# Zero-padded filter operand, a later inverse transform, and GpSimd's share of the norm in a two-layer encoder

## The chip, the cores and the metric

The kernel runs on one core of one Trainium2 chip. The metric is the device time of one execution in microseconds (us): 1728.81 us before, the median of three runs between 1728.32 and 1731.26. Smaller is better.

## The reference

The reference is an encoder of two layers on 256 positions of 1024 channels, in float32. Each layer mixes tokens, adds the result to the stream and normalises, then mixes channels, adds and normalises again:

```
def hybrid_mixer(x, ...):
    proj = einsum('bsd,dp->bsp', x, w_in)                  # 8 x 1024 columns
    a_b, a_c, a_u, h_in, gate_logits = split(proj)
    y_a = a_b * dwconv3_centred(a_c * a_u, conv_a_w)
    h_in = dwconv3_centred(h_in, conv_h_w) + conv_h_b
    h_v, h_x1, h_x0 = split(h_in)
    k_fwd, k_bwd = implicit_filters(...)     # sin-FFN of positions @ w3, times a decay window, unit norm
    z = h_v * h_x1
    z = bidirectional_fft_conv(z, k_fwd, k_bwd) + z * hyena_bias
    y_h = h_x0 * z
    g_a, g_h = split(sigmoid(gate_logits))
    merged = g_a * (y_a @ w_a_out) + g_h * (y_h @ w_h_out)
    return merged @ w_o

def reference(x, ...):
    h = layer_norm(x, ln_in_g, ln_in_b)
    for l in range(2):
        h = layer_norm(ALPHA * h + hybrid_mixer(h, ...), ln_mix_g[l], ln_mix_b[l])
        f = swiglu(h, ...) if l == 0 else moe_swiglu(h, ...)    # dense, then top 2 of 8 experts
        h = layer_norm(ALPHA * h + f, ln_ffn_g[l], ln_ffn_b[l])
    return h
```

A layer_norm subtracts the mean over the 1024 channels, multiplies by 1/sqrt(variance + 1e-5), then by g, and adds b.

## The kernel before

**Matrix products.** Most products are made in three parts (`mm3`, L174 to L176): both operands are split into a rounded high part and a low remainder, and the three matmuls high x high, low x high and high x low add up in one PSUM bank. Weights arrive by SyncE's DMA queue in tiles `wt` of 1 MB. ACT writes the high half of each (L167), VectorE subtracts it for the low half (L168), into a ring `hl` of six tiles of 128x1024; the splitting runs up to five tiles ahead of TensorE. A *chunk* uses two of these tiles: 16 `mm3`, which is 48 matmuls of 128x256. The tiles are numbered here from the start of the kernel (tile 45, tile 46, ...).

**One layer's mixer.** After the norm, `to_T` transposes the 256x1024 stream on TensorE (L542, eight 128x128 blocks for each half `tt` of 128 positions), ACT and VectorE evict with gain and bias (L555, L552), and `hilo` makes the parts `xh` and `xl`. Then come chunks: the inputs of the Hyena branch first, then four `x0_chunk` and twelve `a_chunk`. The discrete Fourier transform of the Hyena branch, its product with the filter and the inverse transform are cut into events (`dft_a`, `dft_b`, `dft_c`, `idft`, each for half 0 or 1 of the channels), and a table `after` says behind which of these 16 chunks each event is issued: the offset `o` plus the place in a list. `dft_c` adds and subtracts on GpSimd and splits the four results on ACT and VectorE (L168, tile `big`). `idft` is 32 matmuls (L705 to L708) whose banks VectorE evicts (L711, L714). After the 16 chunks come four rounds of four chunks (gate, projection of y_a, gate, projection of y_h) and `w_o`.

**The filters.** `flt_c` is called eight times a layer. Each call makes two products of the hidden layer with `w3`: a matmul of 128 rows (L405: the high part twice, against the high and the low part of `w3`) and one of 64 rows (L406: the low part `fl` against the high part of `w3`), for each of the two directions. Layer 0's calls stand among its own chunks; layer 1's stand among layer 0's last chunks, in the stretch of the norm behind layer 0's mixer, and in layer 0's channel mixer.

**The norm.** For each half `tt`, VectorE makes the statistics (L485 to L489), GpSimd raises to -1/2 (L490, called pow below), VectorE applies mean and scale in two pieces of 128x512 (L497). `h_from_n` then makes the stream for the residual on GpSimd: a multiplication (L527) and an addition (L528) of 128x1024 for each `tt`. It does so under `tc.issue_after`, a context of the scheduler in which an instruction is put behind the named one. The norms are numbered by `i`: 0 of the input, 1 and 2 of layer 0, 3 and 4 of layer 1. `to_T` makes parts (`want_parts`) for norms 0 to 2; for norm 3 it does not, and issues `warm(8)` and `warm(2)` behind its two groups of transposes. `warm(n)` is n matmuls of a matrix of ones (L244, 128x512, bfloat16) into a bank that nobody reads.

The order of instructions on each engine is the order in which the program issues them, as a scheduler arranges it at build time.

Of the kernel before, what the change touches and what calls it, by code (L numbers as in the profile page):

```python
# [9 lines left out]
F32 = mybir.dt.float32  # L10
F32R = mybir.dt.float32r
BF16 = mybir.dt.bfloat16
I32 = mybir.dt.int32
U32 = mybir.dt.uint32
AF = mybir.ActivationFunctionType
ALU = mybir.AluOpType

P = 128
S = 256
# [146 lines left out]
def hilo(nc, hi, lo, src):  # L166
    a = nc.scalar.activation(hi, src, AF.Copy)  # L167
    v = nc.vector.tensor_tensor(out=lo, in0=src, in1=hi.bitcast(F32), op=ALU.subtract)  # L168
    return a.ins, v.ins
# [44 lines left out]
def body(tc, nc, x, vec, rows, fg, winT, zT, fw1, fw2, fb, fw3, w_in, w_ao, w_ho, w_o, w13, w2,  # L214
         m13, m2, cst, out, dbg=None):
# [7 lines left out]
    def mm_bank(shape=(P, 2, 256)):  # L223
        t = psum.tile(list(shape), F32, name="mm", tag="mm", bufs=3)
        return t

    def acc_bank(shape=(P, 512)):
        t = psum.tile(list(shape), F32, name="acc", tag="acc", bufs=4)
        return t
# [5 lines left out]
    def warm(n, after=None):  # L235

        if not n:
            return
        t = mm_bank([P, 4, P])
        with ExitStack() as st:  # L240
            if after is not None:
                st.enter_context(tc.issue_after(after.ins))
            for _ in range(n):
                nc.tensor.matmul(t, ones_b, ones_b[:, None, :].to_broadcast([P, 4, P]), start=True, stop=True)  # L244
# [7 lines left out]
    xp = mix.enter_context(tc.tile_pool(name="xp", bufs=1))  # L252
    tmp = mix.enter_context(tc.tile_pool(name="tmp", bufs=10))

    def big8(shape, dt=F32):
        t = big.tile(list(shape), dt, name="big", tag="big")
        return t

    def t2k(shape=(P, 2, 256), dt=F32):
        t = tmp.tile(list(shape), dt, name="t2k", tag="t2k")  # L260
        return t
# [31 lines left out]
    W = Weights(tc, nc, wts, hls, 3, NH - 1)  # L293
# [40 lines left out]
    W.load(3)  # L334
    ff = xp.tile([P, 2, 4, P], F32R)
    gg = xp.tile([P, 4, 2, P], F32R)
    fg_raw = big8([P, 2, 4, P])
    nc.sync.dma_start(fg_raw, fg)

# [17 lines left out]
    def flt_bank(l, shape=(P, 2, 256)):  # L357
        return acc_bank(shape) if l == 0 else mm_bank(shape)

    def flt_h(l, which):  # L360

        n = 64 * (1 + which)
        if which == 0:
            flt_load(l, 0)
            flt_load(l, 1)
            lhs, rhs = fw1_s[:, l], zT_s
        else:
            lhs, rhs = fw2_s[:, l], fs.pop((l, "h"))
        ps = flt_bank(l, [n, S])
        nc.tensor.matmul(ps, lhs, rhs, start=True, stop=True)  # L370
        t = xp.tile([n, S], F32, name="fh", tag="fh")
        sin_of((ps, t, 2 * which, n), l)
        if which == 0:
            fs[l, "h"] = t
        else:
            fs[l] = xp.tile([P, S], F32R, name="fr", tag="fr"), xp.tile([64, S], F32R, name="fl", tag="fl")
            nc.scalar.activation(fs[l][0], t, AF.Copy)
            nc.vector.tensor_tensor(out=fs[l][1], in0=t[:64], in1=fs[l][0][:64].bitcast(F32), op=ALU.subtract)

    def flt_load(l, ct):  # L380
        if ct < 8:
            wn = tmp.tile([P, S], F32, name="wn", tag="wn", bufs=3)
            nc.sync.dma_start(wn, winT[ct])
            w3 = tmp.tile([P, 2, P], F32, name="w3", tag="w3", bufs=2)
            nc.sync.dma_start(w3, fw3[l, ct])
            fs[l, "w", ct] = wn, w3

    def flt_w(l, ct):

        if (l, "w", ct) in fs:  # L390
            wn, w3 = fs.pop((l, "w", ct))
            wr = tmp.tile([P, 2, P], F32R, name="wr", tag="wr", bufs=2)
            with tc.issue_after(last["sina"].ins):
                nc.scalar.activation(wr, w3, AF.Copy)
            nc.vector.tensor_tensor(out=wr[64:], in0=w3[64:], in1=wr[64:].bitcast(F32), op=ALU.subtract)
            fs[l, "p", ct] = wn, wr
            flt_load(l, ct + 2)

    def flt_c(l, ct):

        flt_w(l, ct)
        wn, wr = fs.pop((l, "p", ct))
        ps = flt_bank(l)
        for s in range(2):
            nc.tensor.matmul(ps[:, s], wr[:, s], fs[l][0], start=True, stop=False)  # L405
            nc.tensor.matmul(ps[:, s], wr[:64, s], fs[l][1], start=False, stop=True)  # L406
        if ct != 4 or l == 0:
            flt_w(l, ct + 1)
        hw = t2k()
        nc.vector.tensor_tensor(out=hw, in0=ps, in1=wn[:, None, :].to_broadcast([P, 2, S]), op=ALU.mult)  # L410
        ss = small.tile([P, 2], F32, name="ss", tag="ss")
        sd = t2k()
        for s in range(2):
            nc.scalar.activation(sd[:, s], hw[:, s], AF.Square, accum_out=ss[:, s:s + 1])
        rn = small.tile([P, 2], F32, name="rn", tag="rn")
        nc.gpsimd.tensor_scalar(out=rn, in0=ss, scalar1=1e-6, scalar2=None, op0=ALU.add)
        nc.gpsimd.tensor_tensor(out=rn, in0=rn, in1=mhalf, op=ALU.pow)
        for s in range(2):
            nc.scalar.activation(hw[:, s], hw[:, s], AF.Copy, scale=rn[:, s:s + 1])
        nc.gpsimd.memset(hw[:, 1, 0:1], 0.0)  # L420
        for s, op in enumerate((ALU.add, ALU.subtract)):
            nc.gpsimd.tensor_tensor(out=sd[:, s], in0=hw[:, 0], in1=hw[:, 1], op=op)
        fs[l, "sd", ct] = sd
# [44 lines left out]
    fs = {}  # L468
# [10 lines left out]
    last = {}  # L479
# [42 lines left out]

    def h_from_n(i, n):
        g = gb.pop(i)
        with tc.issue_after(last["pow"].ins):
            for tt in range(2):
                nc.gpsimd.tensor_tensor(out=h_t[:, tt], in0=n[:, tt], in1=g[:, 0], op=ALU.mult)  # L527
                nc.gpsimd.tensor_tensor(out=h_t[:, tt], in0=h_t[:, tt], in1=g[:, 1], op=ALU.add)  # L528

    def to_T(i, n, want_parts=True):  # L530

        xf = big8([P, KT, S])
        xh = xl = None
        if want_parts:
            xh = hp.tile([P, KT, S], F32R, name="xh", tag="xh")
            xl = hp.tile([P, KT, S], F32R, name="xl", tag="xl")
        tbs = [acc_bank([P, 2, 2, P]) for _ in range(4)]
        for tt in range(2):
            for kp in range(4):
                for k in range(2):  # L540
                    kk = 2 * kp + k
                    ins = nc.tensor.transpose(tbs[kp][:, k, tt], n[:, tt, kk * P:(kk + 1) * P], id_s)  # L542
            if not want_parts:
                warm((8, 2)[tt], ins)
        for kp in range(4):
            tb = tbs[kp]
            k0 = 2 * kp
            for k in range(2):
                kk = k0 + k
                g, b = ln_g(i)[:, kk:kk + 1], ln_b(i)[:, kk:kk + 1]  # L550
                if kp % 2:
                    ev = nc.vector.tensor_scalar(out=xf[:, kk], in0=tb[:, k], scalar1=g, scalar2=b, op0=ALU.mult,  # L552
                                                 op1=ALU.add)
                else:
                    ea = nc.scalar.activation(xf[:, kk], tb[:, k], AF.Identity, bias=b, scale=g)  # L555
            if want_parts:
                W.after = hilo(nc, xh[:, k0:k0 + 2], xl[:, k0:k0 + 2], xf[:, k0:k0 + 2])
        if not want_parts:
            W.after = ea.ins, ev.ins
        return xf, xh, xl  # L560
# [40 lines left out]
    def mixer(l, xh, xl):  # L601
# [21 lines left out]
        for j in range(4):  # L623
            ps = proj(W.next(), xs)
# [7 lines left out]
            ps = proj(W.next(), xs)  # L632
# [111 lines left out]

        sts = [{} for _ in range(4)]
        chunks = [(x0_chunk, j) for j in range(4)] + [(a_chunk, j, w, sts[j]) for j, w in A_ORDER]
        o = 5 if l == 0 else 1
        after = {1: [(z_parts, 3)]}
        for q, ev in enumerate(([(dft_a, 0)], [(dft_b, 0, 0)], [(dft_b, 0, 1)], [(dft_a, 1), (dft_c, 0)], [(dft_b, 1, 0)],
                                [(dft_b, 1, 1), (idft, 0)], [], [(dft_c, 1)], [], [(idft, 1)])):  # L750
            after[o + q] = after.get(o + q, []) + ev
        for q, (f, *a) in enumerate(chunks):
            f(*a)
# [22 lines left out]
        for j in range(4):  # L776
            ps = proj(W.next(), xs)
# [3 lines left out]
            ps = proj(W.next(), yas)  # L781
            nc.vector.tensor_tensor(out=ga, in0=ps, in1=ga, op=ALU.mult)
            fill0()
            ps = proj(W.next(), xs)
# [3 lines left out]
            ps = proj(W.next(), yhs)  # L788
# [52 lines left out]
    xf, xh, xl = to_T(0, n_t)  # L841
    W.split(2)
    with W.behind():
        flt_h(0, 0)
# [9 lines left out]
    for l in range(DEPTH):  # L854
# [14 lines left out]
        if l == 0:  # L869
# [3 lines left out]
            xf, xh, xl = to_T(li, n_t)  # L873
# [16 lines left out]
            xf, xh, xl = to_T(li, n_t)  # L890
# [56 lines left out]
    ins = logits(1)  # L947
# [3 lines left out]
    with tc.issue_after(ins.ins):  # L951
        back = [turn_back(0, 1)]
        for tt in range(2):
            ins = nc.tensor.transpose(lgp[:, tt], lgs[:, tt * P:(tt + 1) * P], id_s[:NE, :NE])
# [246 lines left out]
    with tc.issue_after(last["oneh"].ins), tc.issue_after(cp.ins):  # L1201
        for tt in range(2):
            ins = h_half(tt, 1, back[tt])
# [27 lines left out]
    for r, v in enumerate(nc.values_load_multi_w_load_instructions(ix[0:1], engines=[mybir.EngineType.SP], min_val=0,  # L1231
# [4 lines left out]
                            in1=keys[:, None, :].to_broadcast([P, NE, NE]), op=ALU.is_equal)  # L1236
# [155 lines left out]
```

## Time and profile before

| | before |
|---|---|
| median of 3 runs | 1728.81 us (1728.32 to 1731.26) |
| the profiled execution | 1726.32 us |
| its span | 1724.4 us |
| TensorE (PE) busy | 1670.5 us, 97% |
| VectorE (DVE) busy | 710.5 us, 41% |
| ScalarE (ACT) busy | 491.7 us, 29% |
| GpSimd (POOL) busy | 180.3 us, 10% |
| mean granted TensorE clock | 0.982 |

The span is what the trace covers; the execution's time lies 1.9 us above it. Shares over the whole span say little here, since the last half of it is the expert layer and the change lies in the first 700 us. In the rows below a matmul's own "us" is longer than the distance to the next one, because matmuls overlap in the array: what a matmul costs is read as the distance between two starts. PEclk is the granted clock as a share of full speed; 0.50 is 1.2 GHz, 1.00 is 2.4 GHz.

### The profile page before, as it was taken

Reading aid. Unit: us, or ns where it says so; the run is one execution under the profiler, and the core shown is the slowest. Engines: PE = TensorE matmul, PEld = TensorE weight load, DVE = VectorE, ACT = ScalarE, POOL = GpSimd, SP = SyncE. Lnnn points to the kernel's source line nnn. Section 1 sums busy time; section 2 is a strip of 40 time slices with the busy share of each in tenths; the row PEclk is TensorE's granted clock in tenths of the full one; section 3 lists DMA queues with packets and bytes.
Section 4 is the critical chain, followed back from the end, with each engine's and each line's share of the span. In section 5 each row is a group of like instructions: output and inputs, shape, how many; then the busy total and the mean of one; then the engine's idle time right before and its main releaser. Section 6 shows DMA issues by size and latency. Waiting matters only on the chain. (4 is left out here: it accounts for less than half of the span.)

```text
span 1724.4 us, 32503 instructions
## 1 busy us (share of the span) xinstructions
PE 1670.5 (97%) x14105; PEld 1091.8 (63%) x14105; DVE 710.5 (41%) x1009; ACT 491.7 (29%) x775; POOL 180.3 (10%) x163
## 2 busy tenths in 40 slices
PE   7999899899998999999999999999999999999996
PEld 6999899799997999999534333343343333434322
DVE  8989865765557899655410110101101011010112
ACT  4763565454543554543110100000001010010110
POOL 3424311210102034000110000000000000000000
PEclk9999999999998999999999999999999999999998
DMA  7443355355452543656698999999999999999993
GB/s 280 161 165 120 144 192 208 122 176 193 173 195 100 194 147 142 250 174 245 248 396 347 399 419 419 420 418 418 368 415 419 419 419 419 373 367 373 418 420 135
DMA packets 73580, 491.91 MB, mean 285 GB/s; under 512 B 8278, under 2 KB 13144, under 8 KB 14808
## 3 DMA queue, kind: packets, MB, share of 16 engines
q1 hardware_dynamic: 73000, 486.63, 71.7%
q0 software_dynamic: 432, 3.15, 0.5%
q8 instruction: 112, 1.84, 0.4%
q14 instruction: 36, 0.29, 0.0%
HBM read 488.70 MB, written 1.05 MB: 284 GB/s over the span
## 5 line engine op out<-in xcount | busy, mean ns | idle before, releaser
L1047 PE MATMUL mm<-wt,xe 128*32 128x512 f32 (+1 forms) x3664 | 473.5, 542 | 0.0
L176 PE MATMUL mm<-xh,hl 128*128 128x256 f32 x1376 | 393.0, 286 | 5.9 <-DVE hl L168 5.9
L174 PE MATMUL mm<-xh,hl 128*128 128x256 f32 x1376 | 394.4, 287 | 2.0 <-ACT xh L167 1.1
L175 PE MATMUL mm<-xl,hl 128*128 128x256 f32 x1376 | 393.2, 286 | 2.9 <-DVE xl L168 2.7
L168 DVE TENSOR_TENSOR hl<-wt,hl 128x1024 fp32r<-128x1024 f32 x234 | 305.7, 1311 | 145.2 <-ACT hl L167 144.4
L1047 PE MATMUL mm<-big,xe 128*32 128x512 f32 (+1 forms) x1712 | 295.9, 535 | 0.0
L167 ACT ACTIVATE hl<-wt 128x1024 fp32r<-128x1024 f32 x234 | 245.1, 1054 | 172.5 <-PE mm L176 97.4
L1047 PEld LDWEIGHTS mm<-wt,xe 128*32 128x32 f32 x3664 | 155.7, 110 | 210.9 <-issue 189.9
L176 PEld LDWEIGHTS mm<-xh,hl 128*128 128x128 f32 x1376 | 267.4, 194 | 6.4 <-DVE hl L168 6.3
L174 PEld LDWEIGHTS mm<-xh,hl 128*128 128x128 f32 x1376 | 267.6, 195 | 5.4 <-ACT xh L167 1.9
L175 PEld LDWEIGHTS mm<-xl,hl 128*128 128x128 f32 x1376 | 267.1, 194 | 4.9 <-DVE xl L168 3.9
L1057 DVE TENSOR_TENSOR act<-mm,act 128x512 f32<-128x512 f32 (+1 forms) x32 | 20.0, 625 | 483.4 <-PE mm L1047 483.4
L1096 PE MATMUL acc<-wt,at 128*32 128x512 f32 x1232 | 192.8, 593 | 0.0
L1047 PEld LDWEIGHTS mm<-big,xe 128*32 128x32 f32 x1712 | 86.4, 110 | 101.9 <-issue 91.4
L1056 ACT ACTIVATE act<-mm 128x512 f32<-128x512 f32 (+1 forms) x32 | 17.4, 544 | 457.0 <-PE mm L1047 457.0
L490 POOL TENSOR_TENSOR rs<-rs,mhalf 128x1 f32<-128x1 f32 x10 | 6.8, 675 | 1076.9 <-DVE rs L489 1076.9
L1096 PEld LDWEIGHTS acc<-wt,at 128*32 128x32 f32 x1232 | 53.1, 110 | 83.7 <-issue 82.9
L1096 PE MATMUL acc<-big,at 128*32 128x512 f32 x544 | 101.3, 593 | 0.0
L1101 PE MATMUL acc<-wt,bt 128*32 128x512 f32 x352 | 100.2, 592 | 0.0
L174 PE MATMUL mm<-big,hl 128*128 128x256 f32 x256 | 72.5, 283 | 0.0
L176 PE MATMUL mm<-big,hl 128*128 128x256 f32 x256 | 72.3, 282 | 0.0
L175 PE MATMUL mm<-big,hl 128*128 128x256 f32 x256 | 72.2, 282 | 0.0
(249 smaller groups left out, 1811.3 us busy)
## 6 DMA issues: line engine op xcount, KB each, us to landing
wt<-in_m_dram SPq DMA_DIRECT2D x231, 1024.0 KB, 12.6
big<-in_m_dram SPq DMA_DIRECT2D x103, 1024.0 KB, 13.3
wt<-in_w_in_dram SPq DMA_DIRECT2D x62, 1024.0 KB, 4.8
wt<-in_w_dram SPq DMA_DIRECT2D x33, 1024.0 KB, 4.9
wt<-in_w_ho_dram SPq DMA_DIRECT2D x8, 1024.0 KB, 5.7
wt<-in_w_ao_dram SPq DMA_DIRECT2D x7, 1024.0 KB, 4.8
wt<-in_w_o_dram SPq DMA_DIRECT2D x6, 1024.0 KB, 4.9
big<-in_rows_dram POOLq DMA_DIRECT2D x3, 1024.0 KB, 7.7
```

The costliest lines, as they stand in the source:

```text
L167: a = nc.scalar.activation(hi, src, AF.Copy)
L168: v = nc.vector.tensor_tensor(out=lo, in0=src, in1=hi.bitcast(F32), op=ALU.subtract)
L174: nc.tensor.matmul(out, ah, bh, start=start, stop=False)
L175: nc.tensor.matmul(out, ah, bl, start=False, stop=False)
L176: nc.tensor.matmul(out, al, bh, start=False, stop=stop)
L490: last["pow"] = nc.gpsimd.tensor_tensor(out=rs, in0=rs, in1=mhalf[:, 0:1], op=ALU.pow)
L1047: nc.tensor.matmul(banks[r][32 * q:32 * q + 32, :n], xe[:, k, 32 * sg:32 * sg + 32], cols(w, b, q4), start=k == 0, stop=k == KT - 1, tile_ ...
L1056: nc.scalar.activation(a[:, :n], banks[0][:, :n], AF.Silu)
L1057: nc.vector.tensor_tensor(out=a[:, :n], in0=banks[1][:, :n], in1=a[:, :n], op=ALU.mult)
L1096: nc.tensor.matmul(ya[32 * q:32 * q + 32], at[:, f, 64 * b + 32 * sg:64 * b + 32 * sg + 32], ch[b][0][:, h * D + db * 512:h * D + (db + 1) ...
L1101: nc.tensor.matmul(yb[32 * q:32 * q + 32], bt[:, f, 32 * b:32 * b + 32], ch[b][0][:, h * D + db * 512:h * D + (db + 1) * 512], start=first ...
```

## The change

It has four parts.

1. The low part `fl` of the filters' hidden layer becomes one tile of 128 rows for both layers. Rows 64 to 127 are set to zero once by VectorE, and L406's matmul takes 128 rows in place of 64.
2. `h_from_n` names `last["xl"]`, the last low part of `to_T`, in place of `last["pow"]` in its `tc.issue_after`.
3. `to_T` issues products of ones behind its transposes in norms 0 to 2 too: 8 behind the first half, 10 behind the second.
4. The offset `o` of layer 0's events falls from 5 to 4, and `idft` of half 1 stands two places later in the list: in layer 0 all events come one chunk earlier, and `idft` of half 1 one chunk later; in layer 1 only `idft` of half 1 moves, by two chunks.

```
+    fl = xp.tile([P, S], F32R)
+    nc.vector.memset(fl[64:].bitcast(U32), 0)
...
-            fs[l] = xp.tile([P, S], F32R, name="fr", tag="fr"), xp.tile([64, S], F32R, name="fl", tag="fl")
+            fs[l] = xp.tile([P, S], F32R, name="fr", tag="fr"), fl
             nc.scalar.activation(fs[l][0], t, AF.Copy)
-            nc.vector.tensor_tensor(out=fs[l][1], in0=t[:64], in1=fs[l][0][:64].bitcast(F32), op=ALU.subtract)
+            nc.vector.tensor_tensor(out=fl[:64], in0=t[:64], in1=fs[l][0][:64].bitcast(F32), op=ALU.subtract)
...
-            nc.tensor.matmul(ps[:, s], wr[:64, s], fs[l][1], start=False, stop=True)
+            nc.tensor.matmul(ps[:, s], wr[:, s], fs[l][1], start=False, stop=True)
...
     def h_from_n(i, n):
         g = gb.pop(i)
-        with tc.issue_after(last["pow"].ins):
+        with tc.issue_after(last["xl"]):
...
-            if not want_parts:
-                warm((8, 2)[tt], ins)
+            warm((8, 10 if want_parts else 2)[tt], ins)
...
                 W.after = hilo(nc, xh[:, k0:k0 + 2], xl[:, k0:k0 + 2], xf[:, k0:k0 + 2])
+                last["xl"] = W.after[1]
...
-        o = 5 if l == 0 else 1
+        o = 4 if l == 0 else 1
         after = {1: [(z_parts, 3)]}
         for q, ev in enumerate(([(dft_a, 0)], [(dft_b, 0, 0)], [(dft_b, 0, 1)], [(dft_a, 1), (dft_c, 0)], [(dft_b, 1, 0)],
-                                [(dft_b, 1, 1), (idft, 0)], [], [(dft_c, 1)], [], [(idft, 1)])):
+                                [(dft_b, 1, 1), (idft, 0)], [], [(dft_c, 1)], [], [], [], [(idft, 1)])):
```

Behind line 335 of the kernel before, the lines of the changed kernel are numbered two or three higher (L490 is L493, L527 is L530, L528 is L531, L583 is L586, L731 is L734, L739 is L742).

GpSimd at norm 1: `rs` is the scale of a half, and `h_t` the stream for the residual. Before:

```order
L490 TENSOR_TENSOR rs<-rs,mhalf 128x1 x2
L527 TENSOR_TENSOR h_t<-big 128x1024
L528 TENSOR_TENSOR h_t<-h_t,big 128x1024
L527 TENSOR_TENSOR h_t<-big 128x1024
L528 TENSOR_TENSOR h_t<-h_t,big 128x1024
```

And now:

```order
L493 TENSOR_TENSOR rs<-rs,mhalf 128x1
L530 TENSOR_TENSOR h_t<-big 128x1024
L493 TENSOR_TENSOR rs<-rs,mhalf 128x1
L531 TENSOR_TENSOR h_t<-h_t,big 128x1024
L530 TENSOR_TENSOR h_t<-big 128x1024
L531 TENSOR_TENSOR h_t<-h_t,big 128x1024
```

The first half's multiplication now stands ahead of the second half's pow; none of the four instructions stands behind the low parts, which VectorE makes. Norm 2 reads the same, and norm 0 is unchanged.

VectorE in layer 0 around `idft` of half 1: `hl` is the low half of a weight tile (the first row is tile 45), `big` with 128x512 a low part of `dft_c` or of y_a, L583 and L585 convolution taps, L731 and L739 the products of an `a_chunk`. Before:

```order
L168 TENSOR_TENSOR hl<-wt,hl 128x1024
L583 SCALAR_TENSOR_TENSOR t2k<-t2k,vec_s 128x255 x2
L585 SCALAR_TENSOR_TENSOR t2k<-t2k,vec_s 128x255 x2
L168 TENSOR_TENSOR hl<-wt,hl 128x1024
L739 TENSOR_TENSOR t2k<-mm,t2k 128x512
L168 TENSOR_TENSOR hl<-wt,hl 128x1024
L168 TENSOR_TENSOR big<-t2k,big 128x512 x5
L168 TENSOR_TENSOR hl<-wt,hl 128x1024 x3
L731 TENSOR_TENSOR t2k<-mm,t2k 128x512
L168 TENSOR_TENSOR hl<-wt,hl 128x1024
```

And now:

```order
L168 TENSOR_TENSOR hl<-wt,hl 128x1024
L586 SCALAR_TENSOR_TENSOR t2k<-t2k,vec_s 128x255 x2
L588 SCALAR_TENSOR_TENSOR t2k<-t2k,vec_s 128x255 x2
L168 TENSOR_TENSOR big<-t2k,big 128x512 x4
L168 TENSOR_TENSOR hl<-wt,hl 128x1024
L742 TENSOR_TENSOR t2k<-mm,t2k 128x512
L168 TENSOR_TENSOR hl<-wt,hl 128x1024
L168 TENSOR_TENSOR big<-t2k,big 128x512
L168 TENSOR_TENSOR hl<-wt,hl 128x1024 x3
L734 TENSOR_TENSOR t2k<-mm,t2k 128x512
L168 TENSOR_TENSOR hl<-wt,hl 128x1024
```

The four low parts of `dft_c` of half 1 moved from behind tile 47 to ahead of tile 46. On TensorE, `idft` of half 1 moved from between tiles 45 and 46 to between 47 and 48; in layer 1 it moved from behind tile 191 to behind tile 195.

## Rows read from the trace of the kernel before

**Rows 1.** The page: the span of the profiled execution.
```profile
span 1724.4 us, 32503 instructions
```

**Rows 2.** Waits of PE: line waited, releaser, us in total, times, longest.
```profile
PE acc L542 <- DVE big L497: 10.4, 6, 3.6
PE mm L176 <- DVE hl L168: 5.9, 2, 5.3
```

**Rows 3.** Windows: stretch, length, busy us (and instructions) per engine, PEclk, DMA share, GB/s.
```profile
15.42:18.83 3.41, 3.41 (x18) 3.41 (x17) 3.38 (x6) 2.55 (x3) 0.64 (x1) 0.50 1.01 408
54.00:130.00 76.00, 75.96 (x574) 71.23 (x573) 64.09 (x101) 52.70 (x114) 29.75 (x43) 1.00 0.51 170
161.26:164.92 3.66, 3.66 (x35) 3.66 (x34) 3.66 (x6) 2.95 (x4) 1.61 (x1) 1.00 0.00 0
342.00:346.50 4.50, 4.38 (x20) 4.09 (x20) 4.50 (x8) 2.52 (x5) 1.37 (x1) 0.50 0.02 4
549.17:558.16 8.99, 7.52 (x31) 6.93 (x32) 8.99 (x15) 4.24 (x7) 3.24 (x2) 0.50 0.01 2
900.00:1000.00 100.00, 100.00 (x1000) 37.04 (x998) 9.20 (x19) 9.16 (x18) 1.29 (x1) 1.00 0.93 379
```

**Rows 4.** Timeline of PE at a filter call: start, us, engine, line, tiles.
```profile
241.70 0.28 PE L175 MATMUL mm<-big,hl 128*128 128x256 f32 x1
241.81 0.29 PE L176 MATMUL mm<-big,hl 128*128 128x256 f32 x1
...
242.46 0.38 PE L405 MATMUL mm<-fr,wr 128*128 128x256 f32 x1
242.77 0.38 PE L406 MATMUL mm<-fl,wr 64*128 64x256 f32 x1
```

**Rows 5.** Timeline of PE around layer 0's idft of half 1: before and behind.
```profile
189.00 0.28 PE L176 MATMUL mm<-xh,hl 128*128 128x256 f32 x1
...
200.06 0.28 PE L174 MATMUL mm<-xh,hl 128*128 128x256 f32 x1
```

**Rows 6.** Timeline of DVE, same stretch: tile 46, and five low parts.
```profile
188.35 1.21 DVE L168 TENSOR_TENSOR hl<-wt,hl 128x1024 fp32r<-128x1024 f32 x1
...
191.22 3.09 DVE L168 TENSOR_TENSOR big<-t2k,big 128x512 fp32r<-128x512 f32 x5
```

**Rows 7.** Timeline of PE around layer 1's idft of half 1: before and behind.
```profile
674.91 0.28 PE L176 MATMUL mm<-xh,hl 128*128 128x256 f32 x1
...
685.29 0.28 PE L174 MATMUL mm<-xh,hl 128*128 128x256 f32 x1
```

**Rows 8.** Timeline of DVE in layer 1: tile 194.
```profile
679.91 1.21 DVE L168 TENSOR_TENSOR hl<-wt,hl 128x1024 fp32r<-128x1024 f32 x1
```

**Rows 9.** Timeline of POOL at norm 1: first multiplication and addition.
```profile
333.03 2.33 POOL L527 TENSOR_TENSOR h_t<-big 128x1024 f32<-128x1024 f32 x1
335.44 2.41 POOL L528 TENSOR_TENSOR h_t<-h_t,big 128x1024 f32<-128x1024 f32 x1
```

**Rows 10.** Timeline of DVE at norm 1: both halves' L497, then low parts.
```profile
330.39 1.00 DVE L497 TENSOR_SCALAR big<-big,mv,rs 128x512 f32<-128x512 f32 x2
...
333.10 5.04 DVE L497 TENSOR_SCALAR big<-big,mv,rs 128x512 f32<-128x512 f32 x2 [0.67 <-POOL rs L490]
...
340.26 4.87 DVE L168 TENSOR_TENSOR xl<-big,xh 128x512 fp32r<-128x512 f32 x4
```

**Rows 11.** Timeline of PE at norm 1: second half's transposes, first chunk.
```profile
338.19 1.11 PE L542 MATMUL acc<-id_s,big 128*128 128x128 f32 x4 [1.83 <-DVE big L497]
...
342.00 0.58 PE L174 MATMUL mm<-xh,hl 128*128 128x256 f32 x1
```

**Rows 12.** Timeline of PE at norm 2: first half's transposes, second's first ones.
```profile
540.11 1.11 PE L542 MATMUL acc<-id_s,big 128*128 128x128 f32 x8 [0.21 <-DVE big L497]
544.83 1.12 PE L542 MATMUL acc<-id_s,big 128*128 128x128 f32 x4 [3.61 <-DVE big L497]
```

**Rows 13.** Timeline of PE near the router: six products of ones.
```profile
842.02 1.46 PE L244 MATMUL mm<-ones_b 128*128 128x512 bf16 x6
```

## Prediction

> **What bounds the kernel now.** I read the page first [rows 1]: TensorE is busy 97% of a span of 1724.4 us, so a gain must come from matmuls that take too long or from the few places where TensorE waits. Then the waits of TensorE [rows 2]: the largest releaser is line 497, the norm's application, with 10.4 us; 5.9 us are waits for low halves of weights, of which one of 5.3 us lies behind norm 0. Then windows [rows 3]: behind such waits the granted clock is 0.50 (1.2 GHz) and stays there for 3 to 9 us of the rows shown, where matmuls of 128x256 start about 0.213 us apart instead of 0.12 (3.41 us hold 16 starts, beside two matmuls that run in from its edge). Then the timelines of the places that the change touches. The expert layer from 900 us on has TensorE busy throughout and its DMA share at 0.93 [rows 3]; its weights follow each other into tiles as these come free, so I let what is gained ahead of it pass through whole.
>
> **Part 1, the filters.** At a filter call the matmuls of lines 405 and 406 start 0.31 us apart, while the ones ahead of them, equally of 256 columns, start 0.11 to 0.12 apart [rows 4]. Both lines are slow though only line 406 has 64 rows: a call alternates between 128 and 64 rows, and each change of form costs. With 128 rows throughout I expect 0.12. Eight calls a layer with four matmuls each are 32 in layer 0 and 32 for layer 1, of which eight stand in norm 1 and are counted there. 32 x 0.19 = 6.1, less for a first matmul that starts on time: 6.0. 24 x 0.19 = 4.6, taken as 4.3, since these are more and smaller groups. Bounds: nothing (0.31 stays) to 10.7 us; I take **10.3** by the neighbours in the same rows. VectorE pays one memset, once, while it waits for the input: nothing.
>
> The rows show 0.31 us at 64 rows. The Trainium skill (TensorE: Matmul & The Clock Gate, section "Why this matters for your kernels", row on small-K matmuls) says that a single matmul with 32 rows takes the time of one with 128. By that alone the number of rows buys nothing and this term is 0; by the rows it is 10.3. The page speaks of matmuls of one form, so it does not contradict a cost of alternating; it is why I keep that rival.
>
> **Part 4 in layer 0.** From the end of tile 45 (189.00 + 0.12) to the start of tile 46 at 200.06 TensorE spends 10.94 us [rows 5] on an inverse transform that takes 3.66 us when its operands are there (the short window with clock 1.00 in [rows 3]): 7.3 us lost to waiting for the parts and to the lowered clock that followed. With the transform two tiles later, the parts are there. But VectorE now makes the four low parts ahead of tile 46: 4/5 of 3.09 = 2.5 us [rows 6]. Before, tile 46 was ready at 188.35 + 1.21 = 189.56. VectorE can gain the 6.0 us of the filters, since it is idle 11.9 of the 76 us in which their calls lie [rows 3]; so tile 46 is ready at 189.56 - 6.0 + 2.5 = 186.0. TensorE has ended tile 45 at 183.1 and waits 2.9 us: a wait replaces the wait. Tiles 46 and 47 are a chunk of 5.76, then 3.66 of transform: 195.4. Before, tile 48 was due at 200.06 + 5.76 = 205.8. So 10.4 us by there, 6.0 of them the filters'. A wait of 2.9 may lower the clock again; a stretch like those of rows 3, 3.41 to 8.99 us at 0.213 instead of 0.12, would cost 1.5 to 3.9, of which I charge 0.9. The term is **3.5**, between 0.5 (the longest such stretch) and 7.3 (VectorE never late). The first reader of this transform is the fourth of the following chunks, 17 us on, so nothing waits there.
>
> **Part 4 in layer 1.** From 675.03 to 685.29 are 10.26 us [rows 7], 6.6 more than 3.66. VectorE's order ahead of tile 194 does not change; that tile is ready at 679.91 + 1.21 = 681.12 [rows 8], TensorE would want it at 675.03 + 5.76 = 680.8, and waits 0.3. Less 0.2 for chance: **6.1**, between 3 and 6.6.
>
> **Parts 2 and 3, the norms.** The edit to `h_from_n` does not do what its name says: the four instructions are on GpSimd, the instruction named is VectorE's, and the order shows no place behind the low parts; what is left is that the first multiplication goes ahead of the second pow. At norm 1 VectorE's two pieces of 512 took 5.04 us where the first half's two took 1.00 [rows 10]: each sat out a GpSimd instruction of 2.33 or 2.41 [rows 9]. Now the multiplication runs from 331.39 to 333.7, pow ends by 334.4 (VectorE waited 0.67 for it before [rows 10]), the addition holds the first piece until 336.8, and the second is free: both done by about 337.8 instead of 338.14. So the order alone is worth 0.3, with -0.8 where the second half's statistics are held by the multiplication too.
>
> The row shows VectorE's pieces held for whole GpSimd instructions. The Trainium skill (SBUF — State Buffer, section "Who interferes with whom") says that the two engines share a port pair, locked for a whole instruction, and that a VectorE instruction with at most one SBUF input outside the two-port modes is not held. By it the statistics run beside the multiplication and the order is worth +0.3; without it -0.8.
>
> The products: six took 1.46 us with the last one's tail [rows 13], so 0.22 each at full clock and 0.43 at half. Ten behind the second half's transposes (now ending at 339.0 instead of 339.3 [rows 11]) take 2.2 to 4.3, the eight filter matmuls behind them 1.0 to 1.7, and the first chunk starts between 342.0 and 345.0; before, at 342.00. By 346.5, 18 of its matmuls had started (20 in the window of rows 3, two of them filter matmuls running out). At full clock 37 would have: +2.3 us. At half clock 7: -1.3. In the one stretch with TensorE busy throughout, the half clock lasted 3.41 us (15.42 to 18.83); in those with waits it lasted longer [rows 3]. The products fill what were waits, so I lean to the upper half: **+1.2** at norm 1.
>
> At norm 2 no filter matmuls follow. TensorE's waits of 3.61 us and less remain in part [rows 12], the chunk's first 31 matmuls took 8.99 us [rows 3]; with products it starts at 550.3 to 552.5 instead of 549.17. At full clock 65 would start by 558.16, +4.1; at half 27, -0.5. The low parts take 4.87 us for four [rows 10], which the first matmuls will still meet, so **+2.5**. At norm 0 the eight products push the second half's transposes back by up to 1.7 us, and VectorE's parts behind them; the wait of 5.3 us [rows 2] that follows, ended by VectorE, swallows any gain of TensorE and passes on VectorE's delay: **-0.5**, between -1.7 and 0.
>
> **Sum.** 10.3 + 3.5 + 6.1 + 1.2 + 2.5 - 0.5 = 23.1 us. The profiled execution took 1726.3, so 1703.2 in its terms; the median of the runs lies 2.5 higher, so 1705.7.
>
> **The rivals.**
> A: VectorE is nowhere late and the clock stays up. Terms 10.7, 7.3, 6.6, 2.3, 4.1, 0: 31, so about 1698. For it: VectorE idles 12 us in the filters' stretch. Against it: it was the last to arrive at layer 0's transform, and 2.5 us are put ahead of tile 46.
> B: the norms cost instead of gaining: -1.3, -1, -1.7. Then 16, about 1713. For it: half-clock products take 4.3 us each time. Against it: TensorE stood idle in most of that time.
> C: the filter gain does not reach VectorE, which then makes tile 46 at 192.0; 10.4 becomes 4.4, the sum 17, about 1712. For it: VectorE is 84% busy there. Against it: it works up to five tiles ahead and its idle time is what such a lead leaves.
> D: matmuls of 128 rows against zeros start 0.31 apart too. Then the filter term is gone and the rest stays: 13, about 1716. Against it: every other 128-row matmul of that size in these rows.
> E, slower: the multiplication ahead of the second pow holds the statistics as well, and the products run at half clock behind it: at norms 1 and 2 the second half comes 1.1 us later, 18 products there cost up to 7.7 us at half clock, and the lowered clock lasts on into the chunk: up to 9 us a norm, 18 in all. It decides only where the terms of parts 1 and 4 fall below that, so together with D. For it: the clock was 0.50 in both places. Against it: eight of the 18 fill a wait in any case.
>
> **How the numbers follow.** Chances: the forecast 0.58, A 0.12, B 0.11, C 0.11, D 0.05, E 0.03. The likeliest is 1705.7. The range takes in A's edge, B and C and leaves out D and E: 1697.5 to 1714.5. A difference below 0.2% (3.5 us) cannot be told from none: all cases but E lie beyond it; with a little for D and E together, faster 0.94, same 0.03, slower 0.03.
>
> **What would show it.** Filters: lines 408 and 409 start 0.12 apart. Layer 0: the wait at lines 708 to 711 is gone and one of about 3 us for a low half stands in the two chunks ahead. Layer 1: no wait at the transform, 6 us. Norms: L500's second half takes about 3.4 instead of 5.04 us, and the clock behind the products is up within one chunk. I am wrong if the starts stay 0.31 apart, if TensorE waits more than 5 us for tiles 41 to 47, or if norms 1 and 2 end later than before.

## The result and the profile after

The changed kernel takes 1706.57 us, median of four runs (1706.11 to 1709.31), beside 1728.62 for the kernel before in the same comparison: a ratio of 0.9872 with the interval 0.9855 to 0.9889, so 22 us (19 to 25) faster. The forecast was 1705.7. The first line of the profile's page, and of the waits of TensorE those that count (line, releaser, us in total, times, longest), of the changed kernel:

```profile
span 1705.1 us, 32624 instructions
...
PE mm L176 <- DVE hl L168: 9.1, 5, 4.9
PE acc L545 <- DVE big L500: 6.6, 4, 3.2
PE mm L174 <- DVE t2k L742: 2.3, 2, 1.4
...
PE acc L408 <- DVE wr L398: 0.6, 1, 0.6
```

Against [rows 1] the span is 19.3 us shorter, less than the medians say; why comes below. Against [rows 2] the norm's wait fell from 10.4 to 6.6, and the wait for low halves of weights rose from 5.9 to 9.1. Most of that, 7.6 us, still lies behind norm 0 (it was 5.9 there), and only 1.5 us lie in layer 0's transforms, where a new wait was forecast; 1.4 of the 2.3 us for L742 stand beside them.

Both kernels use the weight tiles in the same order, so the start of the first matmul on a tile, before minus after, tells what has been gained up to there, and the difference between two tiles what the stage between them gained. From the timelines of the profiled executions (the last column is a second profile of the changed kernel, from the experiments):

| stage (between tiles) | forecast | changed | again |
|---|---|---|---|
| norm 0 (to 10) | -0.5 | -1.2 | -0.7 |
| filter calls of layer 0 (10 to 25) | 6.0 | 4.8 | 4.8 |
| transforms of layer 0 (25 to 50) | 3.5 | 2.7 | 2.7 |
| filter calls of layer 1 (50 to 83, 125 to 131) | 4.3 | 4.7 | 4.4 |
| norm 1 (83 to 95) | 1.2 | 1.1 | 1.3 |
| norm 2 (149 to 161) | 2.5 | 2.7 | 2.7 |
| transform of layer 1 (161 to 197) | 6.1 | 5.5 | 5.5 |
| all, to the last tile before the experts (239) | 23.1 | 20.25 | 20.7 |
| the expert layer and the end | 0 | -0.9 | -0.7 |

**Filter calls.** The timeline of TensorE of the changed kernel at the call of [rows 4]:

```profile
235.62 0.28 PE L408 MATMUL mm<-fr,wr 128*128 128x256 f32 x1
235.74 0.28 PE L409 MATMUL mm<-fl,wr 128*128 128x256 f32 x1
235.85 0.28 PE L408 MATMUL mm<-fr,wr 128*128 128x256 f32 x1
```

The starts are 0.12 apart instead of 0.31, on both lines though only one was changed.

**Layer 0's transform.** TensorE, then VectorE's tile 46, in the changed kernel:

```profile
173.55 0.39 PE L176 MATMUL mm<-xh,hl 128*128 128x256 f32 x1 [1.33 <-DVE hl L168]
...
190.01 0.36 PE L174 MATMUL mm<-xh,hl 128*128 128x256 f32 x1 [1.37 <-DVE t2k L742]
...
195.84 0.28 PE L708 MATMUL acc<-gg,big 128*128 128x256 f32 x1
...
199.50 0.28 PE L174 MATMUL mm<-xh,hl 128*128 128x256 f32 x1
```

```profile
188.05 1.21 DVE L168 TENSOR_TENSOR hl<-wt,hl 128x1024 fp32r<-128x1024 f32 x1
```

The transform itself runs in 3.66 us without a wait, against 10.94 in [rows 5]. In its place TensorE waits at tiles 41 and 46 for VectorE, whose tile 46 is ready at 189.26; before it was 189.56 [rows 6], and 186.0 was forecast. The granted clock is 1.00 from 171 to 200 us. A third place stands earlier, at the first event (`dft_a` of half 0), which now comes a chunk earlier, behind tile 25. There, between 116 and 120 us, TensorE waits three times for VectorE, 1.3 us in all, which it did not in the kernel before. Of its waits between 110 and 225 us:

```profile
PE acc L174 <- DVE big L168: 1.1, 2, 0.7
PE acc L174 <- DVE big L464: 0.2, 1, 0.2
```

**Layer 1's transform.** It stands a chunk later and still ends at 676.55 (685.29 in [rows 7]). TensorE waits 0.91 us ahead of tile 194:

```profile
667.08 0.35 PE L174 MATMUL mm<-xh,hl 128*128 128x256 f32 x1 [0.91 <-DVE t2k L742]
...
676.55 0.28 PE L174 MATMUL mm<-xh,hl 128*128 128x256 f32 x1
```

**Norm 1.** GpSimd, VectorE and TensorE of the changed kernel:

```profile
322.05 2.36 POOL L530 TENSOR_TENSOR h_t<-big 128x1024 f32<-128x1024 f32 x1 [1.12 <-DVE big L500]
324.37 0.55 POOL L493 TENSOR_TENSOR rs<-rs,mhalf 128x1 f32<-128x1 f32 x1
324.90 2.33 POOL L531 TENSOR_TENSOR h_t<-h_t,big 128x1024 f32<-128x1024 f32 x1
...
330.49 3.62 POOL L531 TENSOR_TENSOR h_t<-h_t,big 128x1024 f32<-128x1024 f32 x1
```

```profile
321.89 0.68 DVE L488 BATCH_NORM_STATS2 st<-big 128x6 f32<-128x512 f32 x1
322.61 0.21 DVE L490 BATCH_NORM_AGGREGATE mv<-st 128x2 f32<-128x12 f32 x1
322.85 0.15 DVE L492 TENSOR_SCALAR rs<-mv 128x1 f32<-128x1 f32 x1
324.96 3.01 DVE L500 TENSOR_SCALAR big<-big,mv,rs 128x512 f32<-128x512 f32 x2 [1.96 <-POOL rs L493]
...
330.55 4.70 DVE L168 TENSOR_TENSOR xl<-big,xh 128x512 fp32r<-128x512 f32 x4
```

```profile
327.58 1.97 PE L545 MATMUL acc<-id_s,big 128*128 128x128 f32 x8 [2.66 <-DVE big L500]
329.34 2.94 PE L244 MATMUL mm<-ones_b 128*128 128x512 bf16 x10
...
333.07 0.28 PE L174 MATMUL mm<-xh,hl 128*128 128x256 f32 x1
...
335.31 0.39 PE L175 MATMUL mm<-xl,hl 128*128 128x256 f32 x1 [0.52 <-DVE xl L168]
```

The multiplication goes ahead of pow, the statistics run beside it unhindered, and only one of L500's two pieces is held: 3.01 us where [rows 10] has 5.04. The second half's eight transposes follow in one go instead of two [rows 11]. The first chunk, however, waits at 335.31 for the later ones of its four low parts (`xl`), whatever came ahead of it: the third of them takes 2.8 us instead of 0.7, beside GpSimd's last addition, and the fourth ends at 335.25.

### The profile page after: what moved, and what is told of

Same layout as the page of the kernel before. It is cut to its first block, busy times and chain, and to the rows that moved or that the text cites. A ratio compares the mean times of both kernels' runs of the same rounds, so it can differ in the third digit from the quotient of the medians.

```text
span 1705.1 us, 32624 instructions
## 1 busy us (share of the span) xinstructions
PE 1658.0 (97%) x14159; PEld 1079.9 (63%) x14159; DVE 703.9 (41%) x1010; ACT 489.5 (29%) x775; POOL 185.1 (11%) x163
## 5 line engine op out<-in xcount | busy, mean ns | idle before, releaser
L176 PEld LDWEIGHTS mm<-xh,hl 128*128 128x128 f32 x1376 | 264.4, 192 | 10.1 <-DVE hl L168 10.1
L174 PEld LDWEIGHTS mm<-xh,hl 128*128 128x128 f32 x1376 | 264.5, 192 | 4.6 <-issue 3.1
L493 POOL TENSOR_TENSOR rs<-rs,mhalf 128x1 f32<-128x1 f32 x10 | 6.8, 676 | 1058.6 <-DVE rs L492 1058.6
```

The costliest lines, as they stand in the source:

```text
L174: nc.tensor.matmul(out, ah, bh, start=start, stop=False)
L176: nc.tensor.matmul(out, al, bh, start=False, stop=stop)
L493: last["pow"] = nc.gpsimd.tensor_tensor(out=rs, in0=rs, in1=mhalf[:, 0:1], op=ALU.pow)
```

## The experiments

All start from the changed kernel. Gains are starts of tiles against the profile of the kernel before, unless a time is named. The first seven were run once each, beside single runs of the kernel before (1728.86 us for e1 to e4, 1726.71 for e5 to e7); e8 to e10 were run four times.

**e1_rows64**: the filters with 64 rows.

```
-            nc.tensor.matmul(ps[:, s], wr[:, s], fs[l][1], start=False, stop=True)
+            nc.tensor.matmul(ps[:, s], wr[:64, s], fs[l][1][:64], start=False, stop=True)
```

Expected: 

> The changed kernel with the 64-row filter matmul back. Theory 1: in layer 0 VectorE sets the pace by itself from tile 5 to tile 46 (its tiles were ready 1.2 us later than before throughout, although TensorE had gained 4.8 us by tile 25), so tiles 5 to 45 are ready at the same times as in the changed kernel, TensorE's lead over VectorE merely grows by 4.8 us, the waits at tiles 41 to 46 shrink, and tile 48 starts within 1 us of 199.5; only layer 1's filter calls (3.1 us between tiles 59 and 83, 1.6 us at tile 131 and some 2 at norm 1) come back: about 6 us slower in all. Theory 2: the filter gain reaches VectorE through the ring and counts whole: tile 48 starts 4.8 us later, 11 us slower in all. A third: 64 rows were not the cause, the starts stay 0.12 apart and nothing changes.

Measured: 1712.31 us. The filter calls of layer 0 gain nothing at all now (the gain is -0.31 us at tile 10 and -0.30 at tile 25), so the rows of one line made both slow; layer 1's 4.7 us are gone too, and the gain at tile 239 falls from 20.25 to 13.76. Norm 1, which holds eight of these matmuls, gains 1.4 us all the same. But tile 48 starts only 1.8 us later than in the changed kernel, not 4.8. VectorE's tile 46, of this run:

```profile
189.89 1.21 DVE L168 TENSOR_TENSOR hl<-wt,hl 128x1024 fp32r<-128x1024 f32 x1
```

It is ready at 191.10, against 189.26 with the filters' gain. Up to tile 26 VectorE's tiles keep a constant distance to the changed kernel's (0.9 us earlier, the two runs' difference at norm 0), though TensorE is up to 3.9 us later here; between tiles 27 and 31, where VectorE waits for products of the transforms, it falls 2.7 us behind. So theory 1 holds up to tile 26, and of the 4.8 us 2.7 reach VectorE behind it. TensorE itself loses the other 2.1 at `dft_a` behind tile 25, where this run has no wait and the changed kernel has three: this run is 3.9 us later at tile 25 and 1.8 at tile 26. Why VectorE gained nothing up to tile 26, the trace of the kernel before says. Its waits between 40 and 112 us:

```profile
DVE hl L168 <- ACT hl L167: 4.4, 4, 1.9
DVE t2k L583 <- ACT t2k L591: 3.5, 4, 1.2
DVE t2k L410 <- PE acc L406: 0.5, 1, 0.5
```

and those of ACT there, between 54 and 112:

```profile
ACT t2k L419 <- POOL rn L417: 8.1, 7, 1.6
ACT t2k L414 <- DVE t2k L410: 4.6, 4, 2.3
ACT big L591 <- PE mm L176: 2.1, 3, 0.9
```

VectorE waits for ACT, and ACT for GpSimd and VectorE, which make the filters' norm between them; TensorE hardly stands in this ring, so a faster TensorE gives VectorE nothing there.

**e2_noprod** and **e3_powedge**: without the products at norms 0 to 2, and with GpSimd's order of before.

```
-            warm((8, 10 if want_parts else 2)[tt], ins)
+            warm((0 if want_parts else 8, 0 if want_parts else 2)[tt], ins)
```

```
-        with tc.issue_after(last["xl"]):
+        with tc.issue_after(last["pow"].ins):
```

Expected: 

> The changed kernel without the products of ones at norms 0 to 2, GpSimd's order kept. Theory 1: the products are what won at norms 1 and 2 by keeping the clock up: there the gain falls from 1.1 and 2.7 us to 0.3 or so each (the order alone), and at norm 0 the 1.2 us lost come back except some 0.5 that are the input's later arrival: 3.2 us lost and 0.7 won, 2.5 us slower. Theory 2: the order of GpSimd won, the products only fill: norms 1 and 2 stay within 0.5 us, norm 0 wins 0.7, so the kernel is a little faster.

Expected: 

> The changed kernel with h_from_n behind pow again, as before; products kept. Theory 1: the order is worth 0.3 us a norm: norm 1 and norm 2 each 0.3 us later than in the changed kernel, 0.6 us in all. Theory 2: with one piece of the norm held by a GpSimd instruction instead of two, less of the clock is lost too: each norm 1.5 to 2 us later, 3 to 4 us in all. Theory 3: the multiplication ahead of pow cost something: each norm earlier by 0.5 or more.

Measured: 1708.88 and 1711.00 us. What each norm gained, with the changed kernel's second profile in the last column:

| | order alone (e2) | products alone (e3) | both | both, again |
|---|---|---|---|---|
| norm 1 | 1.1 | -0.3 | 1.1 | 1.3 |
| norm 2 | 2.2 | 2.0 | 2.7 | 2.7 |

That is theory 2 of e2: the order is what wins. e1 and e5, whose norms are those of the changed kernel, gained 1.4 us at norm 1 and 2.4 at norm 2, so the products add at most 0.3 us at norm 1 and 0.2 to 0.5 at norm 2. Either edit alone does most of norm 2. e3 loses 1.3 and 0.7 us against the changed kernel, which lies between its theories 1 and 2. TensorE at norm 1 without products:

```profile
327.03 1.97 PE L545 MATMUL acc<-id_s,big 128*128 128x128 f32 x8 [4.15 <-DVE big L500]
...
330.08 0.38 PE L174 MATMUL mm<-xh,hl 128*128 128x256 f32 x1
...
334.73 0.39 PE L175 MATMUL mm<-xl,hl 128*128 128x256 f32 x1 [2.29 <-DVE xl L168]
```

The chunk starts 3.0 us earlier than with products, and then waits 2.29 instead of 0.52 for the same low parts; this run is 0.55 us ahead there, so the parts come at the same moment. They are late because GpSimd's last addition holds one of them. Both run times lie some 2 us above what their gains at tile 239 (20.35 and 18.46) say: the expert layer and the end took 907.4 and 907.6 us in these two executions, 905.2 in the changed kernel's. Norm 0 is not decided by e2: its start varies with the run (e10).

**e4_behind**: GpSimd's instructions really behind the low parts, which is what the changed line names.

```
-        with tc.issue_after(last["xl"]):
+        d = small.tile([P, 1], F32, name="hd", tag="hd")
+        with tc.issue_after(last["pow"].ins):
+            ins = nc.gpsimd.tensor_tensor(out=d, in0=last["xlt"][:, KT - 1, S - 1:S].bitcast(F32), in1=mhalf[:, 0:1],
+                                          op=ALU.mult)
+        with tc.issue_after(ins.ins):
```

(`last["xlt"]` is the tile `xl`.) Expected: 

> The changed kernel with the four GpSimd instructions really behind the low parts of the norm: a small GpSimd instruction reads the last low part, and they follow it. Theory 1: GpSimd's multiplication and addition held VectorE's application of the second half (3.0 us for what takes 1.0) and delayed pow by 1.4 us, so the second half's transposes come 3 us earlier at norms 1 and 2, the clock is not lowered, and the first chunk starts 2 to 4 us earlier at each: 4 to 8 us faster. Theory 2: TensorE is then held by the evictions and the products, and later VectorE work that GpSimd now holds (L463, L464) delays the filters: 0 to 2 us faster.

Measured: 1706.52 us, no gain. Yet norm 1 first gains 6.5 us (tile 89) and norm 2 8.2 (tile 157): no piece of L500 is held, and TensorE waits for neither half (0.2 us at norm 2). At norm 1 it is all given back behind the norm, and 2.5 us more; norm 2 keeps 4.6 (the changed kernel has 2.7). GpSimd and VectorE behind norm 1, and TensorE:

```profile
329.09 5.12 POOL L534 TENSOR_TENSOR h_t<-big 128x1024 f32<-128x1024 f32 x2
334.17 5.00 POOL L535 TENSOR_TENSOR h_t<-h_t,big 128x1024 f32<-128x1024 f32 x2
```

```profile
329.33 2.63 DVE L464 TENSOR_TENSOR big<-t2k 128x256 f32<-128x256 f32 x1
331.88 2.60 DVE L463 TENSOR_TENSOR big<-t2k 128x256 f32<-128x256 f32 x1
334.41 2.56 DVE L464 TENSOR_TENSOR big<-t2k 128x256 f32<-128x256 f32 x1
336.89 2.56 DVE L463 TENSOR_TENSOR big<-t2k 128x256 f32<-128x256 f32 x1
339.37 0.41 DVE L464 TENSOR_TENSOR big<-t2k 128x256 f32<-128x256 f32 x1
```

```profile
341.11 0.58 PE L174 MATMUL mm<-xh,hl 128*128 128x256 f32 x1 [7.37 <-DVE t2k L413]
```

Four combinations of 0.41 us take 2.6 each, one GpSimd instruction long, and L413, which frees the bank of a filter call for the next chunk, is queued behind them. That is theory 2.

**e5_o5**: layer 0's offset at 5 again, `idft` of half 1 behind the last chunk.

```
-        o = 4 if l == 0 else 1
+        o = 5 if l == 0 else 1
...
-                                [(dft_b, 1, 1), (idft, 0)], [], [(dft_c, 1)], [], [], [], [(idft, 1)])):
+                                [(dft_b, 1, 1), (idft, 0)], [], [(dft_c, 1)], [], []) + (([(idft, 1)],) if l == 0 else ([], [(idft, 1)]))):
```

Expected: 

> The changed kernel with layer 0's offset at 5 again and idft of half 1 behind the last chunk, still between tiles 47 and 48; VectorE's four low parts of dft_c stand behind tile 47 as before. Theory 1 (the prediction's step): the four low parts ahead of tile 46 cost TensorE a wait; without them tile 46 is ready 2.5 us earlier, at about 187, the waits at tiles 41 to 46 shrink, and tile 48 starts 1 to 2.5 us earlier than the 199.5 of the changed kernel. Theory 2: VectorE's total work to tile 48 is the same, so tile 48 stays within 0.5 us, and the parts come too late for the transform, which then waits 1 to 4 us: equal or slower.

Measured: 1706.82 us. VectorE's tile 46 is 4.0 us earlier than in the changed kernel, and tile 48 starts 4.0 us earlier, of which 0.7 lie in norm 0:

```profile
184.02 1.21 DVE L168 TENSOR_TENSOR hl<-wt,hl 128x1024 fp32r<-128x1024 f32 x1
```

The edit does more than move the four low parts: all other events of layer 0 come a chunk later again too. Of the 3.3 us without norm 0, 1.9 are won at `dft_a`, where TensorE does not wait now, and 1.4 between tiles 41 and 46. And VectorE, which up to tile 26 is 0.5 us behind the kernel before, is 4.3 us ahead of it at every tile from 33 to 51. TensorE has gained 4.4 by tile 25, so with these places of the events the filters' gain does reach VectorE whole. TensorE's waits between 110 and 225 us:

```profile
PE mm L174 <- DVE t2k L348: 1.7, 1, 1.7
PE mm L174 <- DVE t2k L742: 1.0, 1, 1.0
PE mm L174 <- DVE t2k L734: 1.0, 1, 1.0
```

The first is new and stands behind the transform, ahead of tile 52: VectorE has to do the four parts all the same. Of the 4.0 us 2.1 stay, norm 0's 0.7 among them (tile 239 gains 22.3); the time does not show them, because the expert layer was long again (907.2 us). So the gain to tile 48 is larger than theory 1 has it, its step is worth 1.4 us of it at most, and half of it goes to theory 2's work behind tile 48.

**e6_late** and **e7_late_np0**: as e4_behind, at norms 1 and 2 behind the last filter combination; and the same without products at norm 0.

```
+        e = last["xlt"][:, KT - 1, S - 1:S].bitcast(F32) if i == 0 else kern[1, i - 1][:, 1, 1, 511:512]
...
+            ins = nc.gpsimd.tensor_tensor(out=d, in0=e, in1=mhalf[:, 0:1], op=ALU.mult)
```

```
+            warm(((0, 0) if i == 0 else (8, 10) if want_parts else (8, 2))[tt], ins)
```

Expected: 

> As e4_behind, but at norms 1 and 2 the four GpSimd instructions follow the eight filter combinations of VectorE (L463, L464) instead of the last low part. Theory 1: in e4_behind the first chunk behind norms 1 and 2 came 5.4 to 6.5 us earlier than in the changed kernel and all of it went to eight combinations that GpSimd held for a whole instruction each; ahead of GpSimd they take 2.7 us, so most of it stays: 8 to 12 us faster than the changed kernel, about 1696. Theory 2: the next VectorE instructions (the filters' products and the low halves of weights, each then held) give it back again: within 2 us of the changed kernel.

Expected: 

> As e6_late, without the products of ones at norm 0. Theory 1: the eight products between norm 0's two groups of transposes pushed VectorE's chain back, and VectorE sets layer 0's pace: tile 48 starts 0.5 us earlier, as without any products. Theory 2: the delay of norm 0 was the later arrival of the input in that run alone: no difference.

Measured: 1698.23 and 1697.13 us. e6 keeps all of norm 2 (8.2 us between tiles 149 and 161), and loses 5.3 of norm 1's 6.5 between tiles 93 and 96, where TensorE waits 2.5 us for ACT's parts of the channel mixer: GpSimd's four instructions now stand among those of the filter calls, and hold those and VectorE. Theory 1 is right for norm 2 and not for norm 1. e7 is 0.6 to 0.9 us ahead of e6 from norm 0 on, within what norm 0 varies by.

**e8_h_in_ffn** and **e9_best**: at norm 1 GpSimd's instructions wait for a weight tile in the channel mixer; and that with e5's offset.

```
+            if f == 5:
+                hook()
...
-            acc = ffn(xh, xl)
+            acc = ffn(xh, xl, lambda: h_from_n(1, n_mid))
```

Expected: 

> As e7_late_np0, but at norm 1 GpSimd's four instructions come in the dense channel mixer, behind the low half of a weight tile split there, away from the filters' own GpSimd instructions. Theory 1: e7_late_np0 lost 5 us between tiles 91 and 96 because GpSimd's stream shares its queue with the filters' norm and held VectorE's weight halves; in the channel mixer VectorE works 11.7 us ahead and absorbs 10 us of GpSimd: 4 to 5 us faster than e7_late_np0 at tile 107, about 1693. Theory 2: the loss moves along with GpSimd: the same 5 us are lost a few tiles later.

Expected: 

> e8_h_in_ffn with layer 0's offset at 5 as in e5_o5. Theory 1: the two edits are in different stages and add up: 1.4 to 2 us earlier than e8_h_in_ffn from tile 53 on. Theory 2: with the earlier norm 0 of this kernel VectorE is less late, so the offset is worth nothing.

Measured: 1693.82 us (1692.14 to 1694.56) and **1691.42 us** (1691.26 to 1691.56), beside 1729.30 for the kernel before on the same chip, a ratio of 0.9781 (0.9765 to 0.9797). GpSimd of e8 in the channel mixer:

```profile
373.36 0.19 POOL L532 TENSOR_TENSOR hd<-hl,mhalf 128x1 f32<-128x1 f32 x1 [30.92 <-DVE hl L168]
373.50 5.75 POOL L535 TENSOR_TENSOR h_t<-big 128x1024 f32<-128x1024 f32 x2
379.22 5.93 POOL L536 TENSOR_TENSOR h_t<-h_t,big 128x1024 f32<-128x1024 f32 x2
```

TensorE waits for nothing between 320 and 420 us there: norm 1's 6.5 us stay. The 11.7 us of GpSimd cost nothing where VectorE works ahead: its lead over TensorE falls from 11.7 us to 7.2 and does not run out. That is theory 1 of e8. e9 stands 1.8 us ahead of e8 at tile 239, of which 0.6 lie in norm 0; the offset's own 1.2 match e5's 1.3, so the two edits add up, though to less than expected. e9 beats both kernels.

**e10_after_again**: the changed kernel unchanged.

Expected: 

> The changed kernel again, to see how far one profiled execution speaks for the times: the gains by stage (20.25 us by the expert layer) should repeat within 1 us, and only the expert layer's length should vary, between 904 and 907 us as seen so far. If instead the gains by stage vary by 2 us or more, the readings of single profiles are worth less than I took them for.

Measured: 1705.63 us (1704.62 to 1707.70), and the table above: every stage within 0.5 us. Norm 0's column is the only one that follows no edit: by tile 10 the runs stand between -0.3 and -1.8 us, those with products there (five of the experiments and both profiles of the changed kernel: -0.3 to -1.2) no worse than those without (-0.5 to -1.8); all eleven are later than the kernel before in its one profile, so either that one was early or the change costs something there; which of the two stays open. The expert layer and the end took 903.7 to 907.6 us in the twelve profiled executions, with no order by edit; in the three that took over 907 us TensorE waits 1.8 to 2.4 us there for weights that DMA brings, in the shortest not at all.

## Why the prediction was right, point by point

- **Filters**: right. Of the 6.0 us in layer 0 4.8 came; of the rest 0.6 is a wait of TensorE for the weights of one call (L408 for L398) and 0.4 a wait for GpSimd (L437 for L425), both of which the slow matmuls had hidden. Layer 1 gave 4.4 to 4.7 for 4.3. Rival D, that 64 rows were not the cause, is excluded by e1. No run has matmuls of 64 rows alone, so that it is the change between the two forms that costs, and not the short form itself, is argued and not shown. The Trainium skill's row (TensorE: Matmul & The Clock Gate, section "Why this matters for your kernels") on a single matmul of few rows does not cover this sequence: 0.31 us alternating, 0.12 with zeros.
- **Layer 0's transform**: the sum was off by 0.8 us (2.7 for 3.5), and a step was missing. The prediction priced the last transform and its four low parts, and put at nothing that all other events come a chunk earlier too. That costs TensorE a wait at `dft_a`, 1.9 us by the comparison with e5. The step "VectorE can gain the 6.0 us of the filters, since it is idle 11.9 of the 76 us" is right in the end and not for its reason. The idle time was ACT's and GpSimd's doing, and VectorE gained nothing in that stretch; it gained behind it, between tiles 27 and 33, where it waits for TensorE, and in e5 it gained everything. Tile 46 was ready at 189.3 and not at 186.0: 1.2 us of this are norm 0's, 1.2 the filters' (4.8 for 6.0), and the remaining 0.8 lie in the events that moved. Rival C's 192.0 is what e1 shows without the filters' gain (191.1, in a run 0.9 early); its reason, that the gain does not reach VectorE, does not hold: 2.7 us of it do here, and all of it in e5. With norm 0 the forecast to tile 50 was 9.0, and 6.3 came: almost the whole difference between 23.1 and 20.25. The wait forecast ahead of tile 46 came, split over tiles 41 to 46, and the clock stayed up. No run puts only the last transform back, so its own share is read from the two timelines.
- **Layer 1's transform**: right, 5.5 for 6.1; the wait ahead of tile 194 delays the next start by 1.07 us where 0.3 was forecast, since its chunk needs a bank that VectorE empties (L742), later than the weights. Here too the gain is read from the timelines; no run undoes the move.
- **Norms 1 and 2**: the sums were right (1.1 and 2.7 for 1.2 and 2.5), the reason was not, so their agreement is luck. By the prediction the order alone is worth 0.3 and the products make the rest: e2 has it the other way round. The step priced how early the second half is transposed and left out what the chunk waits for next, the low parts beside GpSimd's last addition. That the statistics are not held came as forecast: 0.68, 0.21 and 0.15 us beside the multiplication. The Trainium skill (SBUF — State Buffer, section "Who interferes with whom") says so of a VectorE instruction with at most one SBUF input outside the two-port modes, and the trace agrees. L500, with one input too, was held; by the same section of the Trainium skill its kind, a `tensor_scalar`, can enter a two-port mode.
- **Norm 0**: -0.5 was forecast, because the products push VectorE's parts back; -1.2 and -0.7 came, but runs without the products lose as much (e10). The step is not borne out, and where the loss comes from stays open.
- **"The edit does not do what its name says"**: shown. The order had no such place, and e4 has the other one, with other waits.
- **The total**: the trace has 19.3 us and the medians 22.1. The kernel before was 2.3 us below its median in its profiled execution, the changed one 0.3 above. Stage by stage the forecast was 2.9 us too high up to the experts, and it counted nothing for the expert layer, which took 0.9 more; that it came within 1 us of 1706.57 is luck, worth about 3 us.

## What to carry to other kernels

Before an engine's idle time is counted as room, read who ends it: an engine gains only where it waits for the one that was sped up (here nothing for 16 tiles, then all of it within seven). When one edit moves several pieces of work, price each of them: here the one left out of the sum cost 1.9 us. When GpSimd streams whole tiles, ask which VectorE instructions it will hold, and which wait is queued behind those; put such streams where VectorE works ahead (here 11.7 us of GpSimd then cost nothing, and e8 is 11.8 us faster than the changed kernel measured beside it, 1693.82 and 1705.63 us). And compare profiles stage by stage at equal instructions: single times here differ by up to 4 us in a stage that no edit touched.

## What the runs showed of the hardware that was not expected

A row of four VectorE instructions of 0.41 us took 10.1 us beside four GpSimd instructions of 2.5 to 2.6 us (e4): one VectorE instruction got through for each of GpSimd's. And a price for what [rows 4] showed already: a matmul of 128 rows ahead of or behind one of 64 is slowed as well, 0.31 us from start to start for 0.12, and 56 such matmuls outside norm 1 cost 9.4 us (the changed kernel against e1), while the eight in norm 1 cost nothing, since the chunk behind them waits in any case.
